# Gated DeltaNet in two parts: decay matrices of all heads among the attention, one substitution for all diagonal blocks

## The chip, the core and the metric

The kernel runs on one core of one Trainium2 chip. The metric is the device time of one execution in microseconds (us). The engines are TensorE (PE, with its weight loads shown apart as PEld), VectorE (DVE), ScalarE (ACT), GpSimd (POOL) and SyncE (SP), whose queue issues this kernel's DMAs.

## The reference

One decoder layer for a prompt of 1024 tokens and eight samples of 8 tokens each (64 tokens), model width 1024, all in float32. The layer is a half-step FFN, a mixer, and a second half-step FFN, each between two RMS norms. The mixer:

```python
h = pre2(x); z = h @ w_in                      # one input projection
# branch A: attention over a window of 128, 8 heads of 64, 2 key heads, sinks
# branch B: causal conv of width 4 on q, k, v with SiLU, then gated DeltaNet, 4 heads of 128
m = (sigmoid(gA) * (oA @ w_branch_a) + sigmoid(gB) * (oB @ w_branch_b)) @ w_out
```

For each head and each chunk, DeltaNet computes

```python
gc = jnp.cumsum(g, axis=-1)
decay = exp(where(incl, gc[:, None] - gc[None, :], -inf))
m = where(strict, (k_beta @ k.T) * decay, 0)   # strictly lower triangular
sol = triangular_solve(m + eye, [k_beta * exp(gc), v * beta])
k_cum, v_u = sol
qk = (q @ k.T) * decay
# then chunk by chunk:
v_new = v_u - k_cum @ s
o = (q * exp(gc)) @ s + qk @ v_new
s = s * exp(gc_last) + (k * exp(gc_last - gc)).T @ v_new
```

and a gated RMS norm of o follows. q and k are l2-normalized first.

## The kernel before

Activations lie with features on the partitions and the 1088 tokens along the free axis, cut into three chunks `CH` of 384, 384 and 320 columns. Large products are float32 in three passes over a high and a low part (`gemm`, lines 138 to 140). The program is Python that writes out every instruction. A scheduler orders them when the kernel is built: for each engine it takes the instruction that comes first in the program among those that it holds to be ready, and the order on each engine is then fixed. Tiles of a pool with several buffers are handed out as they come free; the tiles `SL` have one buffer each.

The mixer begins with projections of the attention's k, v and q (`kvq`). What follows is written in this order: `attention_prompt` (16 items, each a block of 128 queries with half of the heads; scores and transposes go to the PSUM rings `ph` and `py` of two banks each), `attention_sample`, and then for each of the four heads its conv units (`conv_unit`: one projection of 128 features in `pa` PSUM, conv taps on DVE, the result into a tile of the head), the z units (`z_unit`), the gate units (`gate_unit`, 16 in all), and `delta_head`. A unit's weights are two raw tiles (four buffers for all units) that are split into eight high and eight low buffers. Heads 0 and 2 work in the eight tiles `HA` and the ring `ph`, heads 1 and 3 in `YA` and `py`. `YA` also holds the attention's q, k and v.

`delta_head` in its steps, by line of the profile:
- `l2` of q and of k (1002, with `colsum_rsqrt` 993 and `newton` 143): squares, sum over the partitions with a product by ones, reciprocal root, one Newton step.
- decay, QK and M for eight chunks of 128 tokens, four at a time, and for the sample's 64 tokens (1051 to 1112). The result M is the strictly triangular matrix of each chunk.
- the 32x32 diagonal blocks of M go to DRAM (`bm`, 1117 to 1121) and come back with one block to a partition, 34 partitions (1123). Its transposes of k and v (1127 to 1132) lie beside that.
- the substitution (1136 to 1145): 31 steps, two DVE instructions each, on 34 partitions.
- the inverse blocks and their transposes go to DRAM and come back into L and U on the diagonal (1146 to 1157), after POOL has set L and U to zero.
- block products make the full inverse of each chunk (1164 to 1195), then the recurrence over eight chunks (1210 to 1233), the sample (1236 to 1269), the gated norm, and a store to `obd` (1275).

The gates' last four units and the output projections follow. These lines set the order of the head work:

```python
    attention_prompt()
    attention_sample()
    conv_head(0, HA)
    z_unit(0)
    delta_head(0, HA, ph)
    z_unit(1)
    conv_head(1, YA)
    delta_head(1, YA, py)
```

Of the kernel before, what the change touches and what calls it, by code (L numbers as in the profile page):

```python
# [7 lines left out]
F32 = mybir.dt.float32  # L8
# [27 lines left out]
def body(ctx: ExitStack, tc: tile.TileContext, d):  # L36
# [23 lines left out]
    bd = [dp.tile([34, 32, 32], F32, tag=f"bd{i}", name=f"bd{i}") for i in range(12)]  # L60
# [120 lines left out]
    def drain(steps):  # L181
        for _ in steps:
            pass
# [701 lines left out]
    def attention_prompt():  # L885
        for it in range(len(items)):
            att_s(it)
            if it > 0:
                att_o(it - 1)
        att_o(len(items) - 1)  # L890
        for t in range(4):
            nc.sync.dma_start(oad[t, :, :NPR], YA[t][:, :NPR])
# [106 lines left out]
        nc.scalar.activation(rr, ve, AF.Abs_reciprocal_sqrt)  # L999
        newton(rr, ve, tmp)  # L1000

    def l2(x, A, l2s, ps):
        colsum_rsqrt(x, A[4], A[3], A[5], A[4], 0.25, ps)
        nc.vector.scalar_tensor_tensor(out=x, in0=x, scalar=-0.25 * l2s, in1=A[5], op0=ALU.mult, op1=ALU.mult)

    def z_unit(h):
        w = unit(U_Z + h, f"z{h}")
# [25 lines left out]
        for c in range(3):  # L1033
            gate_do(i, w, c)

    def delta_head(h, A, ps):
        q, k, v, M, L, U, QK, R = A
        ar = R[:, :NPR].rearrange("p (i c) -> p i c", c=P)
        mq = s2b.tile([P, 2 * NSM], F32, tag="mq", name=f"mq{h}", bufs=2)

        def tile_of(c):
            w = P if c < 8 else NSM
            return w, slice(c * P, c * P + w), c * 4 + h

        l2(q, A, P ** -0.5, ps)
        l2(k, A, 1.0, ps)
        def wide(t, c0):
            return t[:, c0 * P : c0 * P + 512]

        D, E = R[:, 0:512], R[:, 512:1024]  # L1050
        for c0 in (0, 4):
            pr, pq = ps(), ps()
            for i in range(4):
                w, cs, ix = tile_of(c0 + i)
                ps_i = slice(i * P, i * P + P)
                nc.tensor.matmul(pr[:, ps_i], tk["g"][:, ix : ix + 1].to_broadcast([P, P]), cst[:, C_TRI : C_TRI + P], start=True, stop=True)
            for i in range(4):
                w, cs, ix = tile_of(c0 + i)
                nc.tensor.matmul(pq[:, i * P : i * P + P], k[:, cs], q[:, cs], start=True, stop=True)
            for i in range(4):  # L1060
                w, cs, ix = tile_of(c0 + i)
# [12 lines left out]
            pt, pk = ps(), ps()  # L1074
            for i in range(4):
                nc.tensor.transpose(pt[:, i * P : i * P + P], D[:, i * P : i * P + P], ident)
            for i in range(4):
                w, cs, ix = tile_of(c0 + i)
                nc.tensor.matmul(pk[:, i * P : i * P + P], k[:, cs], k[:, cs], start=True, stop=True)
            nc.scalar.copy(D, pt)  # L1080
            for i in range(4):
                w, cs, ix = tile_of(c0 + i)
                nc.vector.scalar_tensor_tensor(
                    out=M[:, cs],
                    in0=pk[:, i * P : i * P + P],
                    scalar=tk["beta"][:, ix : ix + 1],
                    in1=D[:, i * P : i * P + P],
                    op0=ALU.mult,
                    op1=ALU.mult,
                )  # L1090
        for c in range(8, 9):
            w, cs, ix = tile_of(c)
# [16 lines left out]
            nc.scalar.copy(DT, p[:w, 384 : 384 + w])  # L1109
            nc.vector.scalar_tensor_tensor(  # L1110
                out=M[:w, cs], in0=p[:w, 128 : 128 + w], scalar=tk["beta"][:w, ix : ix + 1], in1=DT, op0=ALU.mult, op1=ALU.mult
            )
        M3 = M[:, :NPR].rearrange("p (c s) -> p c s", s=P)
        L3 = L[:, :NPR].rearrange("p (c s) -> p c s", s=P)
        U3 = U[:, :NPR].rearrange("p (c s) -> p c s", s=P)
        bm, bl, bu = bd[3 * h : 3 * h + 3]
        for b in range(4):
            bs = slice(32 * b, 32 * b + 32)
            nc.sync.dma_start(bm[8 * b : 8 * b + 8].rearrange("c r s -> r c s"), M3[bs, :, bs])
        for b in range(2):  # L1120
            nc.sync.dma_start(bm[32 + b], M[32 * b : 32 * b + 32, NPR + 32 * b : NPR + 32 * b + 32])
        Md = R[:34, :NPR].rearrange("p (r s) -> p r s", s=32)
        nc.sync.dma_start(Md, bm)
        Ld = U[:34, :NPR].rearrange("p (r s) -> p r s", s=32)
# [9 lines left out]
        nc.vector.memset(Ld, 0.0)  # L1134
        nc.vector.memset(U[:34, 0:1024:33], 1.0)
        for j in range(31):
            m = 31 - j
            tv = L[:34, : m * (j + 1)].rearrange("p (a b) -> p a b", b=j + 1)
            nc.vector.tensor_tensor(
                out=tv,  # L1140
                in0=Md[:, j + 1 :, j : j + 1].to_broadcast([34, m, j + 1]),
                in1=Ld[:, j : j + 1, 0 : j + 1].to_broadcast([34, m, j + 1]),
                op=ALU.mult,
            )
            nc.vector.tensor_tensor(out=Ld[:, j + 1 :, 0 : j + 1], in0=Ld[:, j + 1 :, 0 : j + 1], in1=tv, op=ALU.subtract)
        nc.sync.dma_start(bl, Ld)
        Ut = Md
        nc.vector.tensor_copy(Ut, Ld.rearrange("p r s -> p s r"))
        nc.sync.dma_start(bu, Ut)
        nc.gpsimd.memset(L, 0.0)  # L1150
        nc.gpsimd.memset(U, 0.0)
        for b in range(4):
            bs = slice(32 * b, 32 * b + 32)
            nc.sync.dma_start(L3[bs, :, bs], bl[8 * b : 8 * b + 8].rearrange("c r s -> r c s"))
            nc.sync.dma_start(U3[bs, :, bs], bu[8 * b : 8 * b + 8].rearrange("c r s -> r c s"))
        for b in range(2):
            nc.sync.dma_start(U[32 * b : 32 * b + 32, NPR + 32 * b : NPR + 32 * b + 32], bu[32 + b])

        def scale_u(c, Ub):
            w, cs, ix = tile_of(c)  # L1160
# [113 lines left out]
        nc.gpsimd.tensor_tensor(out=QK, in0=QK, in1=U, op=ALU.mult)  # L1274
        nc.sync.dma_start(obd[h], QK)

    def conv_head(h, A):
        for j in range(3):
            conv_unit(4 * j + h, A[j])
# [223 lines left out]
```

## Time and profile before

| | |
|---|---|
| median of 3 runs (range) | 2462.92 us (2461.87 to 2465.39) |
| the profiled execution | 2461.62 us, span 2459.8 us |
| PE busy | 2405.7 us |
| PE weight loads busy | 2305.9 us |
| DVE busy | 1750.1 us |
| ACT busy | 1147.1 us |
| POOL busy | 49.2 us |
| DMA | 257.98 MB, mean 105 GB/s |

Busy time is the union of an engine's instructions. Products overlap in the records: one with 384 columns is shown with some 0.33 us while the next one starts 0.17 us later, so a busy PE is not a PE at its peak. A row of groups has line, engine, operation, output and inputs by the program's names, shape, count, busy time and mean; behind the bar the idle time of the engine just before, and what ended it. `s` is any of the `SL` tiles, which `HA` and `YA` consist of.

### The profile page before, as it was taken

To read this page: it belongs to the slowest core of one execution; us is meant where nothing else is said; L and a number is where in the kernel's file an instruction comes from. 1 tells how busy PE (TensorE), PEld (TensorE's weight loads), DVE (VectorE), ACT (ScalarE), POOL (GpSimd) and SP (SyncE) were. 2 spreads that over 40 slices of the span, in tenths; PEclk is the share of its full clock that TensorE was granted. 3 is DMA by queue.
4 is the path that set the end of the run, shared out by engine and by line. 5 is a ranking of instruction groups with operands and counts; after the bars stand their busy time and mean duration, and the time that the engine had idled before them with its cause. 6 is when DMAs were issued, how large, how long until landed. Compare 5 with 4: busy or idle time off the path is not lost.

```text
span 2459.8 us, 39261 instructions
## 1 busy us (share of the span) xinstructions
PE 2405.7 (98%) x14654; PEld 2305.9 (94%) x14654; DVE 1750.1 (71%) x3550; ACT 1147.1 (47%) x2326; POOL 49.2 (2%) x36
## 2 busy tenths in 40 slices
PE   8999999999999999999999999999999999999997
PEld 7999999999998977988898899999989999999997
DVE  8887657757788576888697536655997576676677
ACT  7644423323465388554544333255754333233344
POOL 0000000000000000011001100000000000000000
PEclk9999999999999999999999999999999999999998
DMA  7332212213454302122212344435533122122453
GB/s 268 124 113 86 74 48 86 70 52 112 155 174 145 101 20 82 49 76 73 67 56 70 105 144 149 144 134 174 187 96 97 48 82 78 47 83 80 151 165 133
DMA packets 159759, 257.98 MB, mean 105 GB/s; under 512 B 34800, under 2 KB 65968, under 8 KB 159560
## 3 DMA queue, kind: packets, MB, share of 16 engines
q1 hardware_dynamic: 159568, 255.47, 32.9%
q8 instruction: 115, 1.88, 0.3%
q14 instruction: 76, 0.62, 0.1%
HBM read 219.43 MB, written 36.96 MB: 104 GB/s over the span
## 4 chain that ended last, share of the span: by engine, by line
PE 82%; DVE 9%; DMA 4%; ACT 3%; issue 2%; SPq 0%; DVEq 0%; ACTq 0%
PE pa L138 10%; PE pa L139 10%; PE pa L140 10%; PE pa L462 8%; PE pa L464 7%; PE pa L463 7%; PE py L344 3%; PE py L345 3%; PE ph L345 3%; PE ph L343 3%; PE ph L344 3%; PE py L343 3%; PE po L874 1%; DMA q_da<-in_dn_dram 1%; DVE t L961 1%
## 5 line engine op out<-in xcount | busy, mean ns | idle before, releaser
L462 PE MATMUL pa<-ch,h_c_s 128*128 128x384 f32 x704 | 237.1, 337 | 4.5 <-DVE t L468 3.8
L463 PE MATMUL pa<-cl,h_c_s 128*128 128x384 f32 x704 | 235.9, 335 | 4.7 <-DVE cl L272 4.7
L464 PE MATMUL pa<-ch,l_c_s 128*128 128x384 f32 x704 | 235.8, 335 | 0.0
L468 DVE TENSOR_TENSOR t<-pa,t 128x384 f32<-128x384 f32 x308 | 170.1, 554 | 83.3 <-PE pa L464 82.9
L462 PE MATMUL pa<-ch,h_c_a 128*128 128x384 f32 x528 | 176.9, 335 | 0.9 <-ACT t L380 0.8
L464 PE MATMUL pa<-ch,l_c_a 128*128 128x384 f32 x528 | 176.5, 334 | 0.0
L463 PE MATMUL pa<-cl,h_c_a 128*128 128x384 f32 x528 | 176.5, 334 | 0.0
L111 ACT CAST h_c_a<-r_c_a 128x512 fp32r<-128x512 f32 x132 | 81.8, 620 | 131.1 <-PE pa L463 111.4
L462 PEld LDWEIGHTS pa<-ch,h_c_s 128*128 128x128 f32 x704 | 132.6, 188 | 8.2 <-DVE t L468 7.2
L463 PEld LDWEIGHTS pa<-cl,h_c_s 128*128 128x128 f32 x704 | 132.7, 188 | 4.9 <-DVE cl L272 4.9
L464 PEld LDWEIGHTS pa<-ch,l_c_s 128*128 128x128 f32 x704 | 132.6, 188 | 0.0
L111 ACT CAST h_c_s<-q_c_s 128x512 fp32r<-128x512 f32 x132 | 82.0, 621 | 103.8 <-PE pa L463 93.3
L138 PE MATMUL pa<-xbh,h_ga 128*128 128x384 f32 (+1 forms) x384 | 129.0, 336 | 0.0
L139 PE MATMUL pa<-xbl,h_ga 128*128 128x384 f32 (+1 forms) x384 | 128.6, 335 | 0.0
L140 PE MATMUL pa<-xbh,l_ga 128*128 128x384 f32 (+1 forms) x384 | 128.0, 333 | 0.0
L462 PEld LDWEIGHTS pa<-ch,h_c_a 128*128 128x128 f32 x528 | 99.1, 188 | 2.0 <-ACT t L380 1.2
L463 PEld LDWEIGHTS pa<-cl,h_c_a 128*128 128x128 f32 x528 | 99.1, 188 | 0.0
L464 PEld LDWEIGHTS pa<-ch,l_c_a 128*128 128x128 f32 x528 | 99.1, 188 | 0.0
L139 PE MATMUL pa<-xbl,h_qkv 128*128 128x384 f32 (+1 forms) x288 | 97.7, 339 | 0.0
L138 PE MATMUL pa<-xbh,h_qkv 128*128 128x384 f32 (+1 forms) x288 | 97.4, 338 | 0.0
L140 PE MATMUL pa<-xbh,l_qkv 128*128 128x384 f32 (+1 forms) x288 | 97.0, 337 | 0.0
L111 ACT CAST h_c_s<-r_c_s 128x512 fp32r<-128x512 f32 x44 | 27.4, 623 | 148.2 <-PE pa L463 133.6
(603 smaller groups left out, 7446.8 us busy)
## 6 DMA issues: line engine op xcount, KB each, us to landing
r_c_a<-in_up_dram SPq DMA_DIRECT2D x132, 256.0 KB
q_c_a<-in_up_dram SPq DMA_DIRECT2D x44, 256.0 KB
q_ub<-in_up_dram SPq DMA_DIRECT2D x44, 256.0 KB
r_ub<-in_up_dram SPq DMA_DIRECT2D x44, 256.0 KB
r_ua<-in_up_dram SPq DMA_DIRECT2D x42, 256.0 KB
q_ua<-in_up_dram SPq DMA_DIRECT2D x42, 256.0 KB
r_da<-in_dn_dram SPq DMA_DIRECT2D x40, 256.0 KB
q_da<-in_dn_dram SPq DMA_DIRECT2D x40, 256.0 KB
```

What stands on the lines that cost most here:

```text
L111: nc.scalar.copy(hi, full)
L138: nc.tensor.matmul(ps[:, :n], hi[:, j, :], at(xh, k), start=first, stop=False)
L139: nc.tensor.matmul(ps[:, :n], hi[:, j, :], at(xl, k), start=False, stop=False)
L140: mm = nc.tensor.matmul(ps[:, :n], lo[:, j, :], at(xh, k), start=False, stop=last)
L343: nc.tensor.matmul(ps[:, :n], hi[:, i, :], hh, start=i == 0, stop=False)
L344: nc.tensor.matmul(ps[:, :n], hi[:, i, :], hl, start=False, stop=False)
L345: nc.tensor.matmul(ps[:, :n], lo[:, i, :], hh, start=False, stop=i == len(hs) - 1)
L462: nc.tensor.matmul(ps, wh[:, k, :], xh[:, k, :], start=k == 0, stop=False)
L463: nc.tensor.matmul(ps, wh[:, k, :], xl[:, k, :], start=False, stop=False)
L464: nc.tensor.matmul(ps, wl[:, k, :], xh[:, k, :], start=False, stop=k == 3)
L468: nc.vector.tensor_tensor(out=out, in0=ps, in1=other, op=ALU.add)
L874: nc.tensor.matmul(po[hs, tp2 * 256 : tp2 * 256 + 256], vtok[:, blk * P + hs.start : blk * P + hs.stop], ptb[:, g2 * 512 + h2 * 256 : g2 * ...
```

## The change

`delta_head` is cut in two. `delta_before` does the l2 norms and the matrices for all four heads, one head after the other, in the same six tiles `HB = HA[0:6]` and with both rings in turn (`pb`). It is written among the attention, which now yields after every item: four items, then q's and k's conv unit of a head, then that head's `delta_before`. M, k, q and QK go to DRAM (`md`, `ms`, `kd`, `qd`, `qkd`). After both attentions `invert` runs one substitution over the diagonal blocks of all heads, 32 blocks to a head and so 128 partitions, and a second one of 7 steps over the sample's 8x8 blocks. It reads the blocks from DRAM and writes the inverses and transposes into the diagonal blocks of `ld`, `ud`, `us`, which `clear` has set to zero by twelve DMAs ahead of the attention. `delta_head` then loads k, M, q, QK, U and L from DRAM and goes on with the transposes, as before. v's conv unit stays just ahead of each head.

```diff
+    def clear(z):
+        nc.gpsimd.memset(z, 0.0)
+        for h in range(4):
+            for t in (ld, ud):
+                nc.sync.dma_start(t[h].rearrange("c (e x) -> (c e) x", x=1032), z[:, :1032])
+            nc.sync.dma_start(us[h].rearrange("b (e x) -> (b e) x", x=65), z[:64, :65])
+    def delta_before(h, B, ps):
+        q, k, QK, M, R, _ = B
+        l2(q, B, P ** -0.5, ps)
+        l2(k, B, 1.0, ps)
 ...
-            nc.gpsimd.tensor_tensor(out=mq[:, NSM:], in0=q[:, cs], in1=eR, op=ALU.mult)
+            nc.gpsimd.tensor_tensor(out=q[:, cs], in0=q[:, cs], in1=eR, op=ALU.mult)
 ...
+        nc.sync.dma_start(whole_rows(md[h]), M[:, :NPR].rearrange("p (c s) -> p c s", s=P))
+        nc.sync.dma_start(rows8(ms[h]), M[:NSM, NPR:])
+        nc.sync.dma_start(kd[h], k)
+        nc.sync.dma_start(qd[h], q)
+        nc.sync.dma_start(qkd[h][:, :NPR], QK[:, :NPR])
+        nc.sync.dma_start(qkd[h][:NSM, NPR:], QK[:NSM, NPR:])
+    def invert(Mt, Lt, tt):
+        sm = s2b.tile([32, 192], F32, tag="sm", name="sm")
+        for n, a, b, x, src, blocks, lds, uds in (
+            (32, Mt[:, :1024], Lt[:, :1024], tt, md, blocks32, ld, ud),
+            (8, sm[:, 0:64], sm[:, 64:128], sm[:, 128:192], ms, blocks8, None, us),
+        ):
 ...
+            for h in range(4):
+                nc.sync.dma_start(Md[per * h : per * h + per], blocks(src[h]))
+            nc.vector.memset(b, 0.0)
+            nc.vector.memset(b[:, 0 : n * n : n + 1], 1.0)
+            for j in range(n - 1):
 ...
+            nc.vector.tensor_copy(Md, Ld.rearrange("p r s -> p s r"))
+            for h in range(4):
+                nc.sync.dma_start(blocks(uds[h]), Md[per * h : per * h + per])
+                if lds:
+                    nc.sync.dma_start(blocks(lds[h]), Ld[per * h : per * h + per])
     def delta_head(h, A, ps):
 ...
+        nc.sync.dma_start(k, kd[h])
+        nc.sync.dma_start(M3, whole_rows(md[h]))
+        nc.sync.dma_start(q, qd[h])
+        nc.sync.dma_start(QK[:, :NPR], qkd[h][:, :NPR])
+        nc.sync.dma_start(QK[:NSM, NPR:], qkd[h][:NSM, NPR:])
+        nc.sync.dma_start(U3, whole_rows(ud[h]))
+        nc.sync.dma_start(L3, whole_rows(ld[h]))
+        nc.sync.dma_start(U[:NSM, NPR:], rows8(us[h]))
+        nc.scalar.copy(mq[:, NSM:], q[:, NPR:])
 ...
-        for j in range(31):
-            m = 31 - j
 ...
-        nc.gpsimd.memset(L, 0.0)
-        nc.gpsimd.memset(U, 0.0)
 ...
-    attention_prompt()
+    att = attention_prompt()
+    HB = HA[0:6]
+    clear(HB[5])
+    for h in range(4):
+        take(att, 4)
+        conv_unit(h, HB[0])
+        conv_unit(4 + h, HB[1])
+        delta_before(h, HB, pb)
+    drain(att)
     attention_sample()
-    conv_head(0, HA)
+    conv_unit(8, HA[2])
     z_unit(0)
+    invert(HB[4], HB[5], HB[3])
     delta_head(0, HA, ph)
     z_unit(1)
-    conv_head(1, YA)
+    conv_unit(9, YA[2])
     delta_head(1, YA, py)
     z_unit(2)
     z_unit(3)
     for i in range(0, 2):
         gate_unit(i)
-    conv_head(2, HA)
+    conv_unit(10, HA[2])
     delta_head(2, HA, ph)
     for i in range(2, 4):
         gate_unit(i)
-    conv_head(3, YA)
+    conv_unit(11, YA[2])
     delta_head(3, YA, py)
```

More of the change, by code (lines that the diff above doesn't have):

```diff
@@ L59, in body @@
     zd = dp.tile([4, P, NT], F32, tag="zd", name="zd")
-    bd = [dp.tile([34, 32, 32], F32, tag=f"bd{i}", name=f"bd{i}") for i in range(12)]
+    md, ld, ud = ([dp.tile([8, 4 * 4128], F32, tag=f"{n}{h}", name=f"{n}{h}") for h in range(4)] for n in ("md", "ld", "ud"))
+    ms, us = ([dp.tile([8, 520], F32, tag=f"{n}{h}", name=f"{n}{h}") for h in range(4)] for n in ("ms", "us"))
+    qd, kd, qkd = ([dp.tile([P, NT], F32, tag=f"{n}{h}", name=f"{n}{h}") for h in range(4)] for n in ("qd", "kd", "qkd"))
     yd = [dp.tile([P, 4, width(2)], F32, tag=f"yd{i}", name=f"yd{i}") for i in range(2)]
@@ L889, in attention_prompt @@
                 att_o(it - 1)
+            yield
         att_o(len(items) - 1)
@@ L1000, in colsum_rsqrt, with l2 @@
         newton(rr, ve, tmp)
-    def l2(x, A, l2s, ps):
-        colsum_rsqrt(x, A[4], A[3], A[5], A[4], 0.25, ps)
-        nc.vector.scalar_tensor_tensor(out=x, in0=x, scalar=-0.25 * l2s, in1=A[5], op0=ALU.mult, op1=ALU.mult)
+    def l2(x, B, l2s, ps):
+        colsum_rsqrt(x, B[5], B[3], B[4], B[5], 0.25, ps)
+        nc.vector.scalar_tensor_tensor(out=x, in0=x, scalar=-0.25 * l2s, in1=B[4], op0=ALU.mult, op1=ALU.mult)
     def z_unit(h):
@@ L1034, in gate_unit, with whole_rows, blocks32, rows8 @@
             gate_do(i, w, c)
-    def delta_head(h, A, ps):
-        q, k, v, M, L, U, QK, R = A
-        ar = R[:, :NPR].rearrange("p (i c) -> p i c", c=P)
[L1039 to L1048, printed above, removed]
+    def whole_rows(t):
+        return t[:, : P * P].rearrange("c (r s) -> r c s", s=P)
+    def blocks32(t):
+        return t.rearrange("c (b q) -> (c b) q", q=4128)[:, : 32 * P].rearrange("g (r s) -> g r s", s=P)[:, :, 0:32]
+    def rows8(t):
+        return t.rearrange("b q -> (b q)")[0 : NSM * NSM].rearrange("(r s) -> r s", s=NSM)
+    def blocks8(t):
+        return t[:, : 8 * NSM].rearrange("b (r s) -> b r s", s=NSM)[:, :, 0:8]
+    def wide(t, c0):
+        return t[:, c0 * P : c0 * P + 512]
+    def clear(z):
[4 more added lines that the diff above has]
+            nc.sync.dma_start(us[h].rearrange("b (e x) -> (b e) x", x=65), z[:64, :65])
+    def chunk_of(c, h):
+        w = P if c < 8 else NSM
+        return w, slice(c * P, c * P + w), c * 4 + h
+    def delta_before(h, B, ps):
+        q, k, QK, M, R, _ = B
+        ar = R[:, :NPR].rearrange("p (i c) -> p i c", c=P)
+        l2(q, B, P ** -0.5, ps)
+        l2(k, B, 1.0, ps)
         D, E = R[:, 0:512], R[:, 512:1024]
```

63 lines of the change are left out of this document (25 added, 38 removed).

## The prediction

> **What bounds the kernel now.** I read the page first, then the sums by stretch of time, then groups and single instructions of the stage that the change touches.
>
> ```profile
> span 2459.8 us, 39261 instructions
> PE 2405.7 (98%) x14654; PEld 2305.9 (94%) x14654; DVE 1750.1 (71%) x3550; ACT 1147.1 (47%) x2326; POOL 49.2 (2%) x36
> PE 82%; DVE 9%; DMA 4%; ACT 3%; issue 2%; SPq 0%; DVEq 0%; ACTq 0%
> ```
>
> TensorE (PE) is busy 98% of the span and holds 82% of the chain of waits. The profiled execution took 2461.62 us, its span is 2459.8, and the median of the runs is 2462.92: I sum against 2461.6. The change lies between the first attention product (857 us) and the last gate product (1495 us):
>
> ```profile
> 857.00:970.00 113.00, 111.38 (x668) 80.68 (x669) 79.24 (x239) 95.89 (x308) 0.00 (x0) 1.00 0.11 34
> 970.00:1080.00 110.00, 108.71 (x712) 99.95 (x712) 93.77 (x266) 62.21 (x113) 7.83 (x7) 1.00 0.22 71
> 1080.00:1240.00 160.00, 155.76 (x1016) 137.60 (x1015) 118.91 (x296) 79.97 (x163) 18.83 (x11) 1.00 0.25 75
> 1240.00:1454.00 214.00, 208.91 (x1336) 188.82 (x1335) 148.01 (x384) 96.12 (x193) 22.32 (x15) 0.99 0.26 78
> 1455.00:1495.00 40.00, 40.00 (x247) 40.00 (x246) 17.72 (x34) 16.92 (x36) 0.00 (x0) 1.00 0.68 221
> ```
>
> The columns are PE, weight loads, DVE, ACT, POOL. The first row is the attention: ACT is busy 95.9 of 113 us, more than anywhere else in this stage. In the next three rows (DeltaNet with z and gate units as cover) PE idles only 1.3, 4.2 and 5.1 us. The last row is pure gate work: 247 matmuls in 40 us, 0.162 us each, so a projection unit (24 matmuls for each of 3 column chunks, 72) costs PE 11.7 us. How much of the attention stretch is such work:
>
> ```profile
> L138 PE MATMUL pa<-xbh,h_qkv 128*128 128x384 f32 (+1 forms) x72 | 25.6, 355 | 0.0
> L138 PE MATMUL pa<-xbh,h_z 128*128 128x384 f32 (+1 forms) x23 | 8.3, 362 | 0.0
> ```
>
> Three lines issue such products, so 3 x 95 = 285 matmuls or 46 us: the 16 attention items themselves hold PE for 113 - 46 = 67 us, their stalls included.
>
> ```profile
> L138 PE MATMUL pa<-xbh,h_z x96: 304/334/708, 943.8 to 1069.4; 128*128 128x384 f32 x64, 128*128 128x320 f32 x32
> L138 PE MATMUL pa<-xbh,h_ga x384: 304/334/707, 1069.8 to 1494.9; 128*128 128x384 f32 x128, 128*128 128x320 f32 x64
> ```
>
> The last z product starts at 1069.4 and the first gate product at 1069.8: units run in the order in which the program writes them, one after the other, because their weight slots are handed out in that order. A gate can't jump ahead to fill a hole. That decides what covers the new stage.
>
> **The change, part by part.**
>
> *One substitution for four.*
>
> ```profile
> L1139 DVE TENSOR_TENSOR s<-s,s 34x31 f32<-34x31 f32 (+15 forms) x124 | 43.0, 346 | 1.8 <-DMA s<-bd 0.3
> L1145 DVE TENSOR_TENSOR s<-s,s 34x31 f32<-34x31 f32 (+15 forms) x124 | 40.8, 329 | 1.5
> L1170 PE MATMUL py<-s,s 128*128 128x128 f32 x32 | 4.4, 280 | 2.4 <-DMA s<-bd 2.3
> L1174 PE MATMUL py<-s,s 128*128 128x128 f32 x32 | 4.6, 287 | 1.5 <-ACT s L1171 1.5
> ```
>
> Four chains of 62 DVE instructions, 83.8 us, become one chain of 62 on 128 partitions, by the mean of 0.338 us an estimated 20.9 us if an instruction costs the same on 128 as on 34 (twice that at the outside), and 14 smaller ones for the sample, at most 4.7 us. So DVE is relieved of some 58 us. PE hardly notices: it was covered by z and gate units, and only the idle in the last two rows stands behind the substitution, 3.9 us. I take -3 (bounds 0 and -8).
>
> *Decay matrices among the attention.* l2 of q and k and the matrices of all heads move into the attention, with the eight q and k conv units. They share one set of tiles, so head h+1 can't write its q and k before head h's four stores have landed. PE work is neither added nor removed; what counts is whether PE has enough of it while this chain runs. One pass of the chain, from the second head pair, where DVE is as loaded as it will be:
>
> ```profile
> 1221.00 1.11 ACT L994 ACTIVATE s<-s 128x1088 f32<-128x1088 f32 x1 [2.55 <-DVE s L146]
> 1224.19 0.89 ACT L998 ACTIVATE s<-ph,epsc 128x512 f32<-128x512 f32 x2 [0.17 <-PE ph L997]
> 1225.10 1.28 ACT L999 ACT_TABLE_LOAD   x1
> 1226.39 1.11 ACT L999 ACTIVATE s<-s 128x1088 f32<-128x1088 f32 x1
> 1227.53 1.28 ACT L1028 ACT_TABLE_LOAD   x1
> 1234.79 1.28 DVE L1004 SCALAR_TENSOR_TENSOR s<-s,s 128x1088 f32<-128x1088 f32 x1
> 1248.08 1.13 DVE L1083 SCALAR_TENSOR_TENSOR s<-ph,tk_beta,s 128x128 f32<-128x128 f32 x4
> 1251.89 0.27 DVE L1110 SCALAR_TENSOR_TENSOR s<-ph,tk_beta,s 64x64 f32<-64x64 f32 x1 [1.09 <-ACT s L1109]
> 1234.32 0.55 DVE L953 SCALAR_TENSOR_TENSOR t<-pa,r 128x384 f32<-128x384 f32 x1
> 1242.57 0.55 DVE L989 SCALAR_TENSOR_TENSOR s<-t,t 128x384 f32<-128x384 f32 x1
> 967.83 3.06 SPq L892 DMA_DIRECT2D oad<-s  x4
> 970.00:975.00 5.00, 5.00 (x42) 3.15 (x42) 3.75 (x15) 4.20 (x12) 0.00 (x0) 1.00 1.00 380
> ```
>
> l2 of k runs from 1221.0 to 1236.1, 15 us; M is complete at 1252.2, 31 us after l2(k) began. The first conv chunk passes from eviction (L953) to its last product (L989) in 8 us. Four stores of 512 KB take 3.1 us to issue, and move 380 GB/s while they last. Most of a head's stores can go before M is complete, so I put 5 us behind it (2 at best, 10 if all four go last). A pass is then 8 (conv tail of q) + 15 (l2 of q, beside which k's tail runs) + 31 + 5 = 59 us. The first head adds to its 31 + 5 four attention items (67/4 = 17), two units (23) and some 15 for tail and l2: 91 us. The stage lasts about 91 + 3 x 59 = 268 us.
>
> What PE can do in it:
>
> ```profile
> L997 PE MATMUL py<-s,eye 128*128 128x512 f32 (+1 forms) x36 | 14.0, 503 | 2.6 <-ACT s L994 2.2 <-ACT s L998 0.3
> L997 PE MATMUL ph<-s,eye 128*128 128x512 f32 (+1 forms) x36 | 14.1, 500 | 1.6 <-ACT s L994 1.6
> 1003.93 1.05 PE L1059 MATMUL ph<-s,s 128*128 128x128 f32 x8
> 1004.82 0.60 PE L1076 MATMUL ph<-eye,s 128*128 128x128 f32 x4
> ```
>
> The L997 rows hold twelve colsums, so 28.1/12 = 2.3 us each, 4.7 a head; four k x q products (x8, each shows twice) start 0.89 us before the next group, so the 32 products of a head cost 7.1: 47 us for four heads. With the attention (67), eight conv units (93) and the sample's attention (an estimated 8) that is 215. Beyond it PE can only run ahead until v0's last product stops at a tile that head 3 still holds: with two buffers each for acc and sg, four for pre and three of PSUM, about three units (v0, z0, z1), 35 us. 251 against 268: a hole of **+17 us** that no gate fills, from 0 (the chain 17 us shorter) to about +60 (310 us, if attention and chain delay each other on ACT, DVE and the ph and py banks).
>
> *What the later stage gains.* Of PE's idle behind DeltaNet, two thirds of the L997 idle (2.8 us) leaves the part where PE is the bound. So do many changes between small and wide products:
>
> ```profile
> 1005.17 0.39 PE L140 MATMUL pa<-xbh,l_qkv 128*128 128x320 f32 x1
> 1005.40 0.30 PE L138 MATMUL pa<-xbh,h_qkv 128*128 128x320 f32 x1
> 1005.55 0.31 PE L139 MATMUL pa<-xbl,h_qkv 128*128 128x320 f32 x1
> ```
>
> The first wide product behind a small one takes 0.23 us to the next start, the second 0.15: 0.08 lost for each return, which some 100 returns of l2 and the matrices (an estimate, bounds 50 and 150) make 8 us. I take **-11** together (0 to -18; part of it returns where PE stays full during the first two heads).
>
> *Stores, loads, clearing.* The two memsets a head leave POOL and one comes: no engine waits for them. Twelve clearing DMAs (4.2 MB), stores of M, k, q, QK and loads of k, M, q, QK, U, L (some 0.5 MB each) come onto SP's queue, about 25 MB beside the 34 to 78 GB/s of the rows above, which leaves room below the 380 that the stores reached. The clearing goes ahead of the attention, where conv weights are due, and a reload that lands late holds up what is queued behind its user: copies for L1131 on ACT, M's masking on POOL, then PE's products. The only such row is the 2.3 us at L1170. Eight reloading waits at 0 to 2.3 us, mostly covered by three or more units: **+1** (0 to +18). Behind the stage nothing moves: DeltaNet would end long before the gates do, and gates are PE work either way.
>
> Sum: 2461.6 + 17 - 11 - 3 + 1 = **2465.6**, say 2466.
>
> ACT's table: the fence above shows a switch to the reciprocal root and one back, 1.28 us each. The load starts as the work before it ends (1224.19 + 0.89 = 1225.08) and the next work starts as the load ends (1226.38). Eight pairs move into the attention, already in the 15 us. The Trainium skill, "ScalarE: Activation LUTs", section "What ACT_TABLE_LOAD costs", puts about 1380 ns of drain beside the 1283 of a load. By that, an estimate, 16 x 1.38 = 22 us more of ACT would fall into the chain and the sum would be near 2488; this trace shows no such drain, so I leave it out.
>
> **The rivals.**
>
> *Faster: the attention is a place where PE has room.* Weight loads are busy 80.7 of 113 us there against 40 of 40 under gates, so PE's 111.4 is not dense work, and a second independent chain could fill ACT's and DVE's waits too. It decides if the pass stays under 53 us, which makes 250 and no hole: 2461.6 - 14 + 1 = 2449, down to 2442 with the full relief. For it: DVE has 34 us left of the 113. Against it: ACT has 17, and a head brings two l2 and the exponentials. The Trainium skill, "Perfetto Trace Analysis", section "Identifying the Most-Contended Engine", says that interleaving regimes with different contended engines can help; this is that rule, and the ACT column is where it is weakest here.
>
> *Slower: the serial chain starves PE.* One set of tiles, attention and heads taking the same ph and py banks. At 73 us a pass the stage takes 310 us, the hole is 59, and the time 2461.6 + 59 - 14 + 1 = 2508; up to 2525 with late stores. It decides from about 60 us a pass, where the stage is 271, the hole 20 and the sum +7. For it:
>
> ```profile
> 900.68 1.10 ACT L994 ACTIVATE s<-s 128x1088 f32<-128x1088 f32 x1
> 970.85 1.88 PE L997 MATMUL ph<-s,eye 128*128 128x512 f32 x4
> ```
>
> Head 0's squares for l2 of q are ready at 902, and the product over them starts at 971, when the attention is over: whoever comes later in the order waits for a ph bank. Against it: the heads now come earlier in the order than the later items.
>
> *The DMAs decide.* Reloads land late and what is queued behind their users stands: +18 in place of +1 makes 2483. Against it: only 2.3 us of PE's idle is put down to a DMA.
>
> **How the numbers follow.** About 0.2%, 5 us, is what a measurement of this kernel can tell from no change. The forecast (hole and relief nearly cancel, 2452 to 2480) has 0.40: faster 0.08, same 0.16, slower 0.16. The faster rival has 0.27, the starving one 0.27, the DMA one 0.06 (slower). Faster 0.35, same 0.16, slower 0.49. The range is 2443 to 2512: it takes in most of both rivals.
>
> **What would show it.** Right: gate products still start only after all z; DVE's substitution near 21 us, once; in the last 50 us before it PE idle or weight loads thin, with q and k waiting for a store; after it fewer than 10 us of PE idle; a dense end of gates of over 100 us. Wrong: gates among the attention, or a pass of less than 53 or more than 65 us.

## The result: 1.5% slower, and the profile after

The changed kernel takes 2500.39 us, median of four runs (2495.05 to 2502.41), against 2464.15 for the kernel before in the same comparison (2461.87 to 2467.69). The ratio is 1.0146, 95% interval 1.0132 to 1.016: 36 us slower by the medians. The profiled execution took 2495.05 us, 33 more than the one of before. The time lies inside the predicted range, but 34 us above the forecast, outside the 2452 to 2480 us that the forecast gave itself, and nearest to the starving rival.

Top of the page of the changed kernel:

```profile
span 2493.3 us, 39094 instructions
PE 2419.1 (97%) x14654; PEld 2319.5 (93%) x14654; DVE 1696.0 (68%) x3372; ACT 1149.3 (46%) x2330; POOL 42.3 (2%) x29
```

DVE has lost 54 us of work (1750.1 before), and the span still grew by 33.5. PE's count of instructions is the same. Where the time went is read from sums by stretch; the columns are length, then busy time of PE, weight loads, DVE, ACT and POOL, PE's granted clock, the DMAs' share and GB/s. First the kernel before:

```profile
857.00:960.00 103.00, 101.38 (x598) 73.30 (x598) 76.24 (x230) 88.93 (x289) 0.00 (x0) 1.00 0.07 20
960.00:1060.00 100.00, 99.91 (x668) 90.29 (x667) 77.80 (x232) 57.05 (x116) 5.52 (x4) 1.00 0.25 80
1060.00:1165.00 105.00, 101.17 (x688) 90.03 (x687) 87.77 (x225) 50.36 (x105) 14.50 (x10) 1.00 0.26 77
1165.00:1250.00 85.00, 82.78 (x508) 73.36 (x509) 60.07 (x141) 47.13 (x88) 8.16 (x5) 1.00 0.22 72
1250.00:1345.00 95.00, 92.78 (x611) 86.48 (x610) 78.29 (x230) 48.03 (x93) 9.91 (x8) 1.00 0.22 64
1345.00:1440.00 95.00, 92.74 (x578) 80.33 (x578) 53.16 (x120) 33.67 (x78) 8.35 (x5) 0.98 0.29 89
```

The same stretches of the changed kernel:

```profile
857.00:960.00 103.00, 101.74 (x610) 85.56 (x608) 75.35 (x219) 71.20 (x189) 2.90 (x3) 1.00 0.15 49
960.00:1060.00 100.00, 86.24 (x473) 71.26 (x473) 71.18 (x184) 68.83 (x141) 4.14 (x4) 0.92 0.16 51
1060.00:1165.00 105.00, 91.10 (x591) 73.14 (x590) 74.00 (x216) 66.97 (x165) 4.46 (x5) 0.95 0.33 102
1165.00:1250.00 85.00, 84.77 (x599) 82.01 (x598) 57.55 (x167) 30.38 (x76) 6.48 (x2) 1.00 0.54 153
1250.00:1345.00 95.00, 90.52 (x566) 76.89 (x566) 50.26 (x104) 43.28 (x103) 14.07 (x6) 0.95 0.45 137
1345.00:1440.00 95.00, 94.10 (x586) 81.87 (x586) 45.30 (x94) 42.70 (x85) 8.98 (x4) 1.00 0.36 118
```

The loss lies between 960 and 1165 us, while heads 1 to 3 go through l2 and matrices. In the first three rows PE idles 1.3 + 13.8 + 13.9 = 28.9 us, where before it idled 1.6 + 0.1 + 3.8 = 5.5: 23.4 more. And the granted clock is 0.92 of 100 us and 0.95 of 105, which is worth up to 8 + 5 = 13 us of full speed. Behind 1165 idle is nearly what it was (5.6 against 6.7 us), with a clock of 0.95 in one of the three rows. In the mean of the stage neither ACT (68.8 of 100) nor DVE (71.2) is full: PE waits for a chain, not for an engine that is busy throughout.

Groups of the changed kernel, with first and last start: the units of z and gates, the stores of M, and the substitution:

```profile
L141 PE MATMUL pa<-xbh,h_z x96: 302/334/687, 1080.2 to 1186.6; 128*128 128x384 f32 x64, 128*128 128x320 f32 x32
L141 PE MATMUL pa<-xbh,h_ga x384: 302/334/667, 1187.0 to 1530.0; 128*128 128x384 f32 x128, 128*128 128x320 f32 x64
L1136 SPq DMA_DIRECT2D md<-s x4: 370/373/378, 931.7 to 1133.1; - x4
L1160 DVE TENSOR_TENSOR s<-s,s 128x31 f32<-128x31 f32 (+15 forms) x31 | 12.7, 411 | 0.7
L1166 DVE TENSOR_TENSOR s<-s,s 128x31 f32<-128x31 f32 (+15 forms) x31 | 10.5, 340 | 0.5
```

The first gate product again stands 0.4 us behind the last z product, and that z product now comes at 1186.6 instead of 1069.4. So no gate could fill a pause before 1187, and gates end at 1530.0 where they ended at 1494.9: 35 us later, which is the loss. M is stored four times between 931.7 and 1133.1: a pass of a head takes (1133.1 - 931.7)/3 = 67.1 us. The substitution is done once, 62 instructions of 23.2 us.

What PE waits for between 950 and 1165 in the changed kernel (total, times, longest):

```profile
PE ph L868 <- ACT s L817: 6.2, 2, 3.7
PE py L1082 <- DVE s L1008: 5.2, 2, 4.4
PE ph L1082 <- DVE s L1008: 5.0, 1, 5.0
```

L1008 is the last multiplication of l2, for which k x q (L1082) waits; L868 transposes an attention item's probabilities. None of the shorter waits in this stretch is put down to a DMA either. One such wait, in the order of time, and the sums by stretch around it:

```profile
1050.92 0.31 PE L143 MATMUL pa<-xbh,l_qkv 128*128 128x320 f32 x1
...
1056.20 1.20 PE L1082 MATMUL ph<-s,s 128*128 128x128 f32 x4 [4.97 <-DVE s L1008]
```

```profile
1050.00:1054.00 4.00, 1.23 (x9) 0.96 (x7) 3.06 (x4) 3.39 (x5) 0.00 (x0) 1.00 0.21 66
1054.00:1061.00 7.00, 4.80 (x23) 4.83 (x23) 3.84 (x7) 1.27 (x3) 1.27 (x1) 0.51 0.32 117
```

The last product of a v unit starts at 1050.92 and PE has nothing until 1056.20. The clock falls to half at 1054 and stays there for the rest of the row, so the pause costs more than its 5 us. The Trainium skill, "TensorE: Matmul & The Clock Gate", Part 1, says that the array's clock goes to half after an idle window of some 3.4 us and comes back after as long a stretch of work; 0.51 over seven microseconds behind a pause of 4.97 agrees with that in kind. The lengths here are not quite those: the clock fell some 3 us after the last product ended (1051.2) and was back at 1061, some 5 us after products started again.

### The profile page after: what moved, and what is told of

It is laid out like the page before. It is cut to its first block, busy times and chain, and to the rows that moved or that the text cites. A ratio compares the mean times of both kernels' runs of the same rounds, so it can differ in the third digit from the quotient of the medians.

```text
span 2493.3 us, 39094 instructions
## 1 busy us (share of the span) xinstructions
PE 2419.1 (97%) x14654; PEld 2319.5 (93%) x14654; DVE 1696.0 (68%) x3372; ACT 1149.3 (46%) x2330; POOL 42.3 (2%) x29
## 4 chain that ended last, share of the span: by engine, by line
PE 88%; DVE 5%; DMA 3%; ACT 3%; issue 1%; SPq 0%; DVEq 0%; ACTq 0%
PE pa L141 12%; PE pa L142 12%; PE pa L143 12%; PE pa L465 8%; PE pa L466 8%; PE pa L467 8%; PE py L347 3%; PE py L348 3%; PE py L346 3%; PE ph L348 3%; PE ph L347 3%; PE ph L346 3%; PE po L877 1%; DMA q_da<-in_dn_dram 1%; DMA q_db<-in_dn_dram 1%
```

## The experiments

The first four tell apart what makes the hole: lack of PE work at that place, the order of ring tiles, the single set of tiles, or the substitution. The others ask what the parts are worth once the hole is filled. Kernels of one comparison share the runs of the kernel before, whose median lay between 2460.07 and 2465.84 us.

**Cover for the hole (fill4).** One gate unit is written behind each head's matrices; the later gates move up.

```diff
         delta_before(h, HB, pb)
+        gate_unit(h)
     drain(att)
...
-    for i in range(0, 2):
+    for i in range(4, 6):
...
-    for i in range(2, 4):
+    for i in range(6, 8):
...
-    for i in range(4, 12):
+    for i in range(8, 12):
```

> Edit: one gate unit per head (4 of the 16) is written behind each head's matrices, ahead of the next head's conv units; nothing else moves. Theory A (PE lacks work within reach while the heads pass one after the other through one set of tiles): four units are 47 us of products for a hole that the trace of the changed kernel puts at some 45 us between 960 and 1165 us, so the time falls by 25 to 40 us, to 2460 to 2475, and most half-clock stretches go. Theory B (the loss is waits inside the interleaved chains, in-order PE behind a late ACT or DVE result, whatever the cover): 2490 to 2502. Theory C (the added DMA traffic and SP's queue): no change, 2495 to 2502.

2459.19 us, ratio 0.9987 (0.9973 to 1.0). Sums by stretch of fill4, and two of its groups:

```profile
960.00:1060.00 100.00, 99.80 (x592) 86.38 (x590) 70.94 (x182) 72.43 (x154) 2.90 (x3) 1.00 0.18 61
1060.00:1165.00 105.00, 101.72 (x687) 85.75 (x686) 75.00 (x207) 67.98 (x164) 6.12 (x6) 1.00 0.35 116
1250.00:1345.00 95.00, 90.62 (x604) 77.55 (x603) 52.35 (x110) 47.23 (x117) 14.08 (x6) 0.98 0.47 147
```

```profile
L1136 SPq DMA_DIRECT2D md<-s x4: 370/374/377, 932.9 to 1148.0; - x4
L141 PE MATMUL pa<-xbh,h_ga x384: 302/334/468, 893.5 to 1492.4; 128*128 128x384 f32 x128, 128*128 128x320 f32 x64
```

The passes are longer still (71.7 us, with a gate unit in each), and yet the whole loss is gone: PE is busy 201.5 of 205 us, at clock 1.00, and the gates end at 1492.4. The work of the chain, its stores and its reloads are all still there. So the loss was PE without work at that place in the order, and the hole is the difference of the two ratios, (1.0146 - 0.9987) x 2464 = 39 us.

**Attention items one at a time (fine).** The items are handed out between the steps of a head's matrices instead of four ahead of it.

```diff
     l2(q, B, P ** -0.5, ps)
+    yield
     l2(k, B, 1.0, ps)
+    yield
     for c0 in (0, 4):
...
+            yield
...
-        take(att, 4)
...
-        delta_before(h, HB, pb)
+        for _ in delta_before(h, HB, pb):
+            take(att, 1)
```

> Edit: the attention's items are written one at a time between the four steps of each head's matrices (l2 of q, l2 of k, first four chunks, last four chunks), instead of four at a time ahead of the head. Theory A with the part that the PSUM rings are handed out in the order of the program, so that items wait for the head ahead of them: items now fill the head's waits, a pass (68 us in the trace) falls to 55 to 60 and the time to 2465 to 2485. Theory B: more changes between two chains, 2500 to 2515. Theory C: 2495 to 2502.

2489.78 us, 1.0117 (1.0099 to 1.0135), between the expectations. Handing the items out singly brings about 7 us of the 36 back. Sums of fine:

```profile
960.00:1060.00 100.00, 83.88 (x510) 66.42 (x508) 67.82 (x177) 72.79 (x177) 5.78 (x6) 0.95 0.17 58
1060.00:1165.00 105.00, 93.92 (x615) 78.08 (x615) 78.02 (x243) 66.25 (x163) 3.51 (x3) 0.93 0.35 110
```

Idle is 16.1 + 11.1 = 27.2 us in these rows against 27.7 in the changed kernel: finer mixing moved the pauses and hardly shortened them. But PE starts 1125 products in these rows instead of 1064; at the prediction's 0.162 us for a gate product some 60 more are 10 us, an estimate, so the gain lies in what PE gets done between the pauses.

**Two sets of q and k (qk2).** Heads 1 and 3 get tiles of their own for q and k.

```diff
+    qk2 = [s2b.tile([P, NT], F32, tag=f"qk{i}", name=f"qk{i}") for i in range(2)]
+    HBS = (HB, qk2 + HB[2:6])
     for h in range(4):
...
-        conv_unit(h, HB[0])
-        conv_unit(4 + h, HB[1])
-        delta_before(h, HB, pb)
+        B = HBS[h % 2]
+        conv_unit(h, B[0])
+        conv_unit(4 + h, B[1])
+        delta_before(h, B, pb)
```

> Edit: q and k of heads 1 and 3 get two tiles of their own, so that the conv units of the next head need not wait for the stores of q and k of the head before. Theory A with the one set of tiles as its cause: a pass falls by the conv tail and the stores (13 us of 68) and the time by 25 to 40 us, to 2460 to 2475. If the scratch tiles, the matrices and the PSUM rings hold the heads one behind the other anyway: a pass falls by under 6 us, and the time is 2485 to 2500. Theory C: 2495 to 2502.

2491.07 us, 1.0118 (1.0103 to 1.0133). Stores of M and one sum of qk2:

```profile
L1136 SPq DMA_DIRECT2D md<-s x4: 370/370/383, 932.2 to 1125.0; - x4
```

```profile
1060.00:1165.00 105.00, 81.01 (x517) 62.77 (x515) 63.05 (x198) 57.83 (x152) 4.46 (x5) 0.89 0.38 118
```

A pass is 64.3 us, 3 less. What PE gains early (it can run ahead with the next q and k) it pays between 1060 and 1165: 24.0 us of idle and a clock of 0.89. PE's work is the same in sum, so running ahead only moves the hole.

**The substitution four times (foursub).** The same 31 steps, once for each head on its own 32 partitions.

```diff
-            for j in range(n - 1):
+            for hs in [slice(32 * h, 32 * h + 32) for h in range(4)] if n == 32 else [slice(0, g)]:
+                for j in range(n - 1):
...
-                tv = x[:, : m * (j + 1)].rearrange("p (a b) -> p a b", b=j + 1)
+                    tv = x[hs, : m * (j + 1)].rearrange("p (a b) -> p a b", b=j + 1)
...
```

> Edit: the substitution of the 32x32 blocks runs four times, on the 32 partitions of one head each, instead of once on 128; all else as in the changed kernel. DVE gets three more chains of 62 instructions, some 60 us, between the matrices and the heads. Theory A (PE is covered there by z, v and gate units): the time rises by 0 to 12 us, 2495 to 2512. Rival (DVE's relief is what the change lives on): it rises by 30 to 60 us, 2530 to 2560.

2578.19 us, 1.0476 (1.0461 to 1.0492): by the ratios 81 us behind the changed kernel, far above what I expected. One sum of foursub, its longest wait of PE between 1165 and 1345, and its two groups of the substitution:

```profile
1165.00:1250.00 85.00, 17.69 (x96) 17.00 (x94) 77.35 (x215) 2.81 (x6) 2.60 (x1) 0.62 0.20 62
PE pa L141 <- DVE t L1018: 76.3, 2, 67.1
```

```profile
L1167 DVE TENSOR_TENSOR s<-s,s 32x112 f32<-32x112 f32 (+15 forms) x124 | 43.4, 350 | 3.6
L1161 DVE TENSOR_TENSOR s<-s,s 32x112 f32<-32x112 f32 (+15 forms) x124 | 41.3, 333 | 3.7
```

An instruction on 32 partitions takes about as long as one on 128 (333 and 350 ns against 340 and 411 in the changed kernel, where one of 2.58 us raises the second mean), so the 84.7 us are four times a chain. In the kernel before, as much DVE work (83.8 us) stood in four places, each beside another unit, and PE hardly idled there. Here it stands in one place in front of all four heads. PE works 17.7 of 85 us: the four chains don't wait for each other, DVE is busy 77 of 85 us, and a z unit stands for 67 us because its own DVE step (L1018, which empties its PSUM tile) doesn't come up.

**The same with cover (foursub8).** foursub with a gate unit a head and four more gates ahead of the substitution; the later gates move up.

```diff
         delta_before(h, HB, pb)
+        gate_unit(h)
...
     z_unit(0)
+    for i in range(4, 8):
+        gate_unit(i)
     invert(HB[4], HB[5], HB[3])
...
```

> Edit: four substitutions of 32 partitions instead of one of 128, as in the run that took 78 us more, but with one gate unit per head among the attention and four more ahead of the substitution (8 of the 16 moved). Theory A (the substitution costs what PE cover doesn't hide): 47 us of products stand beside the 62 us longer chain, so it costs 10 to 35 us over the same kernel with one gate unit per head (2459): 2465 to 2495. Rival (DVE's time counts by itself): about 2520 to 2540.

2518.99 us, 1.0234 (1.022 to 1.0248): 1 us below what the rival expected and far outside theory A. By the ratios it is 61 us more than fill4. One sum of foursub8, and its longest wait of PE between 1165 and 1345:

```profile
1165.00:1250.00 85.00, 64.82 (x373) 62.64 (x371) 74.43 (x207) 12.92 (x28) 2.65 (x1) 0.90 0.36 109
PE pa L141 <- DVE t L957: 45.5, 2, 43.3
```

The gates ahead of the substitution bring PE from 17.7 to 64.8 us in this row. Then PE stands for 43.3 us, from 1235.8 to 1279.0, at z products whose PSUM tile a conv step on DVE (L957) has yet to empty, until the chains are nearly done (their last instruction starts at 1282.8). From 1279 to 1345 it is busy 65.3 of 66 us. So units are not what is short here: their DVE steps stand behind the chains.

**Length alone (sub4).** fill4 with the 128-partition substitution done four times over, each from a fresh identity; only the last result is used. One chain of 248 instructions, each waiting for the one before it.

```diff
-            nc.vector.memset(b, 0.0)
-            nc.vector.memset(b[:, 0 : n * n : n + 1], 1.0)
-            for j in range(n - 1):
+            for _ in range(4 if n == 32 else 1):
+                nc.vector.memset(b, 0.0)
+                nc.vector.memset(b[:, 0 : n * n : n + 1], 1.0)
+                for j in range(n - 1):
...
```

> Edit, from the kernel with one gate unit per head: the substitution of the 32x32 blocks is repeated four times on all 128 partitions, each from a fresh identity, so that its chain of dependent instructions is as long (4 x 62) as the four of the kernel before together, but never has more than one instruction ready. In the runs with four independent chains DVE was busy 77 of 85 us and the z units' last DVE steps stood behind them. Theory A1 (the price there was a DVE filled by independent chains, and z's buffers held): with one dependent chain gaps remain for z's steps, PE has the v, z and gate units of some 70 us beside 62 us more of chain, and the time rises by 5 to 30 us, to 2465 to 2490. Rival (the length of the chain in front of the heads is the price): up by 50 to 70 us, 2510 to 2530.

2523.46 us, 1.0242 (1.0225 to 1.0259): by the ratios 63 us more than fill4, as the rival expected. Two sums of sub4, and its groups of the substitution and of the heads' first products:

```profile
1165.00:1250.00 85.00, 84.97 (x541) 83.56 (x542) 78.05 (x241) 23.80 (x51) 2.51 (x1) 1.00 0.39 120
1250.00:1345.00 95.00, 58.04 (x393) 55.91 (x392) 59.92 (x174) 18.67 (x45) 2.34 (x1) 0.80 0.30 77
```

```profile
L1167 DVE TENSOR_TENSOR s<-s,s 128x31 f32<-128x31 f32 (+15 forms) x124 | 42.4, 342 | 3.3
L1161 DVE TENSOR_TENSOR s<-s,s 128x31 f32<-128x31 f32 (+15 forms) x124 | 42.3, 341 | 3.0
```

```profile
L1215 PE MATMUL ph<-s,s 128*128 128x128 f32 x32 | 6.4, 357 | 35.3 <-DMA s<-ud 35.3
```

The chain is 84.7 us of DVE instead of some 21 (62 x 0.342), so it is longer by what the kernel lost. Units run on beside it: PE is busy 84.97 of 85 us in the first row, and no unit waits for DVE as in foursub8. Then the cover is used up and PE idles 37 us, 35.3 of them until the inverse blocks come back (`ud`). So two different waits cost about the same: four independent chains hold back the units' DVE steps (foursub8, 61 us more than fill4), and one chain as long outlasts the units (63 us). A chain in front of all heads spends the stock of cover once. That the changed kernel's own substitution costs little is a matter of its 23 us.

**More gates later (fill4b).** fill4 with two more gates ahead of head 2's v unit.

```diff
-    for i in range(4, 6):
+    for i in range(4, 8):
...
-    for i in range(6, 8):
+    for i in range(8, 10):
...
-    for i in range(8, 12):
+    for i in range(10, 12):
```

> Edit: as with one gate unit per head among the attention, and two more gate units ahead of head 2's v conv unit, from those at the end. That kernel still left PE some 22 us of unused time between 1250 and 1345 us, where two units stand between the recurrences of heads 0 and 1. Theory A (a unit that waits for head 0's tile stops the units behind it, and the cover is short): about half of the 22 us goes, 2445 to 2453. Theory B (waits inside the two recurrences themselves): no change, 2455 to 2463.

2459.62 us, 0.9993 (0.9984 to 1.0002): no gain. The 4.4 us of idle that fill4 has between 1250 and 1345 isn't lack of units. Waits of PE in fill4 between 1200 and 1345:

```profile
PE ph L1238 <- DVE s L1205: 1.8, 1, 1.8
PE py L1286 <- DVE s L1267: 1.8, 1, 1.8
```

They stand inside the first two heads, between products and DVE steps of the same head.

**The substitution alone (twosets4).** From fill4: attention first, as in the kernel before, and the heads in two sets of tiles and rings by turns.

```diff
-        take(att, 4)
-        conv_unit(h, HB[0])
-        conv_unit(4 + h, HB[1])
-        delta_before(h, HB, pb)
+        if h == 0:
+            drain(att)
+            attention_sample()
+        B, ring = ((HB, ph), (YA[0:6], py))[h % 2]
+        conv_unit(h, B[0])
+        conv_unit(4 + h, B[1])
+        delta_before(h, B, ring)
         gate_unit(h)
```

> Edit, from the kernel with one gate unit per head: both attentions run first, and then the matrices of heads 0 and 2 are made in one set of tiles and one PSUM ring, those of heads 1 and 3 in the other set and ring, as in the kernel before; the single substitution, the stores and reloads stay. So this is the substitution alone, without the matrices among the attention. Theory A (the price was one set of tiles and the shared rings, which put the heads one behind the other, and too few units of cover): two heads overlap, the four take some 150 us behind the attention's 113, PE has work for that, and the time is 2455 to 2470, like the kernel before. Rival (placing the matrices among the attention is what pays for stores and reloads): 2475 to 2500.

2461.27 us, 1.0001 (0.9991 to 1.0012). Stores of M and one sum of twosets4:

```profile
L1136 SPq DMA_DIRECT2D md<-s x4: 370/370/378, 1008.2 to 1138.7; - x4
```

```profile
1060.00:1165.00 105.00, 103.47 (x640) 96.57 (x639) 84.14 (x224) 53.24 (x90) 8.59 (x7) 1.00 0.41 128
```

With two sets a pass is 43.5 us and PE is full. One substitution, the stores, the reloads and a gate unit a head together come out even with the kernel before. Whether each of them is free, or a gain of one pays for another, this run doesn't tell.

**Attention first, one set (attfirst4).** From fill4, `take(att, 4)` becomes `drain(att)`.

> Edit, from the kernel with one gate unit per head: the attention's 16 items all run ahead of head 0; the heads then pass through the one set of tiles one after the other. Theory A: without attention a pass takes some 58 us, the stage 113 + 36 + 4 x 58 = some 350 us against 300 us of PE work within reach, so 2490 to 2520. Rival (heads and attention hinder each other in the PSUM rings by more than they cover): 2440 to 2465.

2476.84 us, 1.006 (1.0045 to 1.0075): between the two expectations. Stores of M of attfirst4:

```profile
L1136 SPq DMA_DIRECT2D md<-s x4: 370/370/371, 1000.0 to 1162.3; - x4
```

Without attention items beside it a pass takes 54.1 us, with a gate unit in it, against 67.1 in the changed kernel without one, and 71.7 in fill4, which has the gate unit too. So 13 us of the pass at the least, and 17.6 like with like, come from the attention beside it. But the attention is also cover: taking it away from the heads costs 18 us against fill4.

**Twice the clearing (clear2).** The changed kernel with its twelve clearing DMAs issued twice, 4.2 MB more on SP's queue ahead of the attention.

```diff
     clear(HB[5])
+    clear(HB[5])
```

> Edit: the changed kernel with the twelve clearing DMAs (4.2 MB) issued twice. Theory A: they run under the k, v, q projections, nothing waits for them: 2493 to 2505, as without. Theory C (added DMA traffic and SP's queue cost time): the second copy costs what the first did, 5 to 15 us more, 2503 to 2517.

2494.65 us, 1.0119 (1.0104 to 1.0133). It isn't slower than the changed kernel, so the clearing is not what the change lost by. Later reloads were not tried alone.

**Putting the pieces together (fill4qk, fill4qkfine).** fill4 with the tiles of qk2, and that with the finer attention of fine; no new lines.

> Edit: one gate unit per head among the attention, and q and k of heads 1 and 3 in two tiles of their own. Theory A: with cover the hole is gone already, so the shorter pass of the second edit no longer shows: 2450 to 2460, the same as with cover alone (2459) or up to 8 us less through fewer waits.

> Edit: the same, and the attention's items written one at a time between the steps of the heads. Theory A: as before it, the pass is shorter but PE is already covered: 2445 to 2460. Theory B (more changes between interleaved chains cost PE): 2460 to 2470.

2459.72 us, 0.9982 (0.9971 to 0.9993), and 2460.33 us, 0.9986 (0.9974 to 0.9998). Both stand with fill4. The best of the versions is 0.18% below the kernel before, inside the 0.2% that the prediction called the limit of a measurement.

## Why the prediction was right or wrong

**The bound and the order: right.** Units do run in the written order: gates start 0.4 us behind the last z. PE is starved where the prediction put the hole, and filling that one place takes the loss away (fill4).

**The hole: right in kind, mis-sized, 39 us instead of +17.** This is the term that failed. The pass of one head was put at 59 us; it takes 67.1, which is past the 65 us that the prediction itself named as a sign of being wrong. Its four pieces can be read from the starts of q's conv steps, of the squares (L998) and of the stores of M, as means over heads 1 to 3:

| | put at | changed kernel | attfirst4 |
|---|---|---|---|
| stores of M to the first conv step of the next q | 5 | 6.3 | 5.8 |
| from there to the squares of q | 8 | 21.0 | 8.9 |
| squares of q to squares of k | 15 | 16.4 | 13.8 |
| squares of k to the stores of M | 31 | 23.6 | 25.6 |

So 59 was near 67 partly by luck: one piece was put 13 us too short and another 7.4 too long. The pieces came from the second pair of heads, where no attention ran, and the four attention items that stand among them were counted for the first head alone and put at nothing for the others. In head 1 q's last conv step ends at 949.58, and the squares of it start on ACT 11.5 us later:

```profile
949.10 0.48 DVE L993 SCALAR_TENSOR_TENSOR s<-t,t 128x320 f32<-128x320 f32 x1
961.06 1.10 ACT L998 ACTIVATE s<-s 128x1088 f32<-128x1088 f32 x1
949.60:961.00 11.40, 11.40 (x64) 8.24 (x63) 5.26 (x17) 10.35 (x34) 0.00 (x0) 1.00 0.08 29
```

ACT is busy 10.35 of these 11.4 us, mostly with the exponentials and scalings of attention items (L813 and L817), which stand ahead of the squares in its order. Over the three heads this wait is 8.7 us in the mean, against 0.6 in attfirst4. In fine, where the items are written later, it is 0.5 us, but there squares of k to stores of M takes 33.4 us and the pass 65.0: the items delay the chain wherever they are put. PE is busy in such a wait (11.40 of 11.4); it runs dry later in the pass, when the rest of the chain is still to come.

The first head went the other way: 75 us to its M (931.7 - 857) instead of 86. The stage so lasts about 1133 + 5 - 857 = 281 us and not 268, which by the prediction's own subtraction makes the hole 281 - 251 = 30. What is left of the 39 is put down to the clock, which is argued and not tested alone: the prediction counted a pause at its length, but the granted clock of 0.92 and 0.95 behind the pauses is worth up to 13 us more. By the trace, 23.4 us of added idle and 13 of clock are 37, against the 39 by the ratios. The note that "it decides from about 60 us a pass" was right; the forecast stood 1 us on the other side of its own border. That the time still fell into 2443 to 2512 is owed to a range that was drawn to take in the rivals.

**The relief of the later stage: -11 was not there.** Idle behind 1165 fell only from 6.7 to 5.6 us, and the clock of 0.95 between 1250 and 1345, worth up to 5 us where before lost up to 2 (0.98 from 1345 to 1440), takes that back. With the hole filled the kernel is only (1 - 0.9987) x 2464 = 3 us below before, where -11 - 3 + 1 = -13 was forecast, and with the attention kept apart it is at 1.0001. The weakest part of the term was the 8 us for changes between small and wide products: no row of the trace of before carried their count. The prediction noted that part of the relief returns where PE stays full, as it does in fill4; no run isolates it, so why the 11 us are missing stays open.

**The substitution: its duration right, the ground for its small price only half.** Predicted 20.9 us on 128 partitions, measured 23.2, with one instruction of 2.58 us in it, and 21.1 in fill4. "PE hardly notices" holds for this length. The prediction didn't say that its cover is now spent for all heads at once; foursub and sub4 show what it costs when more of it stands there: 81 us on the changed kernel, 63 on fill4.

**Stores, loads, clearing: right as far as tested.** DMA traffic in the rows above is up to 153 GB/s, and no wait of PE's between 950 and 1165 us is put down to a DMA. clear2 shows no cost of the clearing, and twosets4 none of stores, reloads and single substitution together.

**The table loads: right.** ACT in the changed kernel, in the same pass as the pause above:

```profile
1047.34 0.31 ACT L1002 ACTIVATE s<-ph,epsc 128x64 f32<-128x64 f32 x1
1047.67 1.28 ACT L1003 ACT_TABLE_LOAD   x1
1048.97 1.11 ACT L1003 ACTIVATE s<-s 128x1088 f32<-128x1088 f32 x1
```

The load starts 0.02 us behind the work before it and the next work 0.02 us behind the load: no drain in the chain. The prediction's side estimate of 2488 came nearer to the result than its sum, but for another reason.

**The rivals.** The starving one came true with its mechanism, at 67 us a pass instead of 73. Its ground, that whoever comes later in the order waits, shows at ACT, where q's squares stand behind attention items, more than at a ring bank; with items handed out singly (fine) some 7 us come back. The interleaving rival is refuted as the change was written, since the pass was far from 53 us; with cover in the written order (fill4) the same interleaving at least costs nothing. The rule that the prediction cites for it stands in the Trainium skill, "Perfetto Trace Analysis", under "Optimization Strategy". Here interleaving alone gave 1.0146, and the ACT column, named there as the weak point, was where the chain was held up.

**What stays open.** The order on ACT explains some 8 of the 13 us that attention adds to a pass; that is read from two traces, and no run changed this order alone. Some 4 more lie in the conv steps of q (12.2 us from the first to the last, against 8.2 in attfirst4), and their cause is not known. Why clear2 came out a little below the changed kernel, in another comparison, is not known.

## What to carry to other kernels

Where units run in the order in which they are written, moving a chain of work earlier needs cover written at the same place: here one gate unit a head was the difference between 1.0146 and 0.9987. Merging four chains into one saves instructions, but puts what is left in front of all consumers at once, so weigh its length against the cover that stands at that one place, and ask whether the cover's own steps on the chain's engine still come up. Read a chain's duration beside the work that will run beside it, piece by piece, not from a stage where that work is absent.

## What the runs showed of the hardware that was not expected

A pause of PE costs more than its length, and it need not be a full pause. Two sums of the changed kernel, in the first heads' recurrences:

```profile
1282.00:1286.00 4.00, 2.34 (x18) 2.05 (x19) 3.86 (x10) 0.80 (x3) 1.56 (x1) 1.00 0.77 215
1286.00:1293.00 7.00, 7.00 (x30) 6.30 (x30) 3.47 (x7) 1.87 (x5) 1.90 (x1) 0.52 0.64 196
```

PE was busy 2.34 of 4 us, with no gap longer than 1.7 us, and then ran 7 us at a clock of 0.52. The wide products of 320 columns in that stretch start 0.27 us apart (1289.25 and 1289.52), where the prediction's rows show 0.15. They are shown as busy all the while, so a busy share alone hides this loss: the row is at 7.00 of 7.00.

And a DVE instruction of the substitution costs about the same on 32, 34 and 128 partitions, with the same elements on each: 0.34 us in the mean on 32 (foursub), on 34 (the kernel before) and on 128 (sub4). The changed kernel's 0.37 (23.2/62) has the one instruction of 2.58 us in it.
